# Rotary embedding on one core: the queue on which two small tables are loaded, and their place among the large loads

## Chip, cores, metric

One core of one Trainium2 chip. The metric is the device time of one execution in microseconds (us), median of the runs. All runs quoted are in the fast state; the granted clock was 1.00 in every one of them.

DVE is the vector engine, ACT the scalar engine and SP the sync engine. SP and ACT also issue the DMAs, each on a queue of its own (the SP queue and the Activation queue): in the profile of the kernel before, one queue has 4608 packets (32 loads) and the other 5664 (32 stores and the tables); of the changed kernel, where SP issues the tables, the first has 5664 and the second 4608. Landing times are those that the profile gives. The span is the length of the one profiled execution, a little less than its device time (328.5 of 330.26 us in the kernel before).

## The reference

```python
x: (8, 2048, 16, 64) float32; cos, sin: (2048, 32) float32
x1, x2 = x[..., 0::2], x[..., 1::2]          # pairs
out1 = x1 * cos - x2 * sin
out2 = x1 * sin + x2 * cos                   # cos, sin by position, the same for batch and head
out  = interleave(out1, out2)                # same shape, float32
```

64 MB go in and 64 MB come out; the tables are 256 KB each.

## The kernel before

The work is cut into 32 tiles of 128 partitions x 4096 floats (2 MB). For each tile: a load of x on the SP queue, a cast to bf16 on ACT (`halve`), three DVE operations (`rotate`), a cast back on ACT and a store on the Activation queue (`store`). There are five buffers for x, four for the output and two for each bf16 tile between them.

```python
    cos_t = cos.rearrange("(g p k) c -> p g (k c)", p=P, k=K)   # P=128, K=4: runs of 512 B
    sin_t = sin.rearrange("(g p k) c -> p g (k c)", p=P, k=K)
    xpool = ctx.enter_context(tc.tile_pool(name="xpool", bufs=NX))      # NX = 5
    opool = ctx.enter_context(tc.tile_pool(name="opool", bufs=4))
    ...  # cut: other pools and tiles
    def load(i):
        ...
        nc.sync.dma_start(out=xt, in_=x_t[b, g])
    ...  # cut: halve, rotate
    def store(i):
        ...
        nc.scalar.copy(out=ot, in_=rotated.pop(i))
        nc.scalar.dma_start(out=out_t[b, g], in_=ot)

    with tc.manual_schedule():
        load(0)
        nc.scalar.dma_start(out=cos_sb, in_=cos_t)
        nc.scalar.dma_start(out=sin_sb, in_=sin_t)
        for i in range(1, NX):
            load(i)
        ...  # cut: three DVE operations make s_tab and c_tab from sin_sb and cos_sb
        halve(0)
        for i in range(n):                    # n = 32
            if i + 1 < n:
                halve(i + 1)
            rotate(i)
            store(i)
            if i + NX < n:
                load(i + NX)
```

The trace adds something that the source doesn't say: the sixth and the seventh load of x wait for the tables, with which they share no data. The SP queue waits 20.1 us for cos and 10.8 us for sin, and these loads are issued at 23.46 and 34.66 us, right after cos and sin land (23.43 and 34.61). Why the program waits there is not shown by the runs. The prediction calls these two the lane waits.

## Time and profile before

| | before |
|---|---|
| median time | 329.98 us (329.90 to 330.17) |
| span of the profiled run | 328.5 us |
| DVE, ACT busy | 66%, 70% |
| moved by DMA | 134.76 MB, 410 GB/s over the span |
| cos, sin: issue to landing | 22.7, 33.4 us |
| first store issued | 46.4 us |

The number to look for is DMA traffic over time; the prediction shows the slices and stretches. Here only the waits that change sides later: engine and line, what it waited for, us in total, times, longest.

```profile
ACT ot L91 <- DMA out_dram<-ot: 36.0, 18, 2.3
...
ACT xh L60 <- DMA xt<-in_x_dram: 7.1, 2, 5.6
```

ACT waits mostly for a free output buffer, that is, for a store to land, and hardly ever for x.

### The profile page before, as it was taken

Reading aid. Unit: us, or ns where it says so; the run is one execution under the profiler, and the core shown is the slowest. Engines: PE = TensorE matmul, PEld = TensorE weight load, DVE = VectorE, ACT = ScalarE, POOL = GpSimd, SP = SyncE. Lnnn points to the kernel's source line nnn. Section 1 sums busy time; section 2 is a strip of 40 time slices with the busy share of each in tenths; the row PEclk is TensorE's granted clock in tenths of the full one; section 3 lists DMA queues with packets and bytes.
Section 4 is the critical chain, followed back from the end, with each engine's and each line's share of the span. In section 5 each row is a group of like instructions: output and inputs, shape, how many; then the busy total and the mean of one; then the engine's idle time right before and its main releaser. Section 6 shows DMA issues by size and latency. Waiting matters only on the chain.

```text
span 328.5 us, 334 instructions
## 1 busy us (share of the span) xinstructions
DVE 218.3 (66%) x99; ACT 230.8 (70%) x65; POOL 0.2 (0%) x4
## 2 busy tenths in 40 slices
DVE  0000798899999999866668866667876666876910
ACT  1710079999999999676786676687677678669740
POOL 0000000000000000000000000000000000000000
DMA  7999739999999999999999999999999999999997
GB/s 295 427 423 425 268 140 353 405 427 435 427 435 429 437 425 437 424 435 427 436 427 435 427 435 429 433 429 433 429 433 429 433 429 433 429 435 427 435 427 315
DMA packets 10275, 134.76 MB, mean 410 GB/s; under 512 B 1057, under 2 KB 2081, under 8 KB 2081
## 3 DMA queue, kind: packets, MB, share of 16 engines
q1 hardware_dynamic: 4608, 67.11, 48.7%
q10 hardware_dynamic: 5664, 67.64, 48.4%
q14 instruction: 3, 0.02, 0.0%
HBM read 67.63 MB, written 67.11 MB: 410 GB/s over the span
## 4 chain that ended last, share of the span: by engine, by line
DMA 62%; ACT 24%; issue 5%; DVE 4%; ACTq 1%
DMA out_dram<-ot 52%; ACT ot L91 18%; DMA sin_sb<-in_sin_dram 10%; ACT xh L60 6%; DVE pt L85 1%; DVE qt L79 1%; DVE pt L80 1%; ACTq L92 1%; ACTq L96 0%; DVE s_tab L102 0%; DVE s_tab L103 0%; ACTq L91 0%; DVE c_tab L104 0%
## 5 line engine op out<-in xcount | busy, mean ns | idle before, releaser
L91 ACT CAST ot<-pt 128x4096 f32<-128x4096 bf16 x32 | 115.3, 3604 | 64.7 <-DMA out_dram<-ot 36.0
L60 ACT CAST xh<-xt 128x4096 bf16<-128x4096 f32 x32 | 115.4, 3605 | 19.5 <-ACT ot L91 12.4
L79 DVE TENSOR_TENSOR qt<-xh,s_tab 128x4096 bf16<-128x4096 bf16 x32 | 73.3, 2291 | 59.2 <-ACT xh L60 59.2
L85 DVE TENSOR_TENSOR pt<-pt,qt 128x4096 bf16<-128x4096 bf16 x32 | 73.3, 2292 | 1.1
L80 DVE TENSOR_TENSOR pt<-xh,c_tab 128x4096 bf16<-128x4096 bf16 x32 | 73.1, 2284 | 0.0
L102 DVE CAST s_tab<-sin_sb 128x512 bf16<-128x512 f32 x1 | 0.5, 454 | 34.6 <-DMA sin_sb<-in_sin_dram 34.6
L60 ACT ACT_TABLE_LOAD x1 | 1.3, 1283 | 1.8 <-issue 1.8
L104 DVE CAST c_tab<-cos_sb 128x1024 bf16<-128x1024 f32 x1 | 0.7, 684 | 0.0
L103 DVE TENSOR_SCALAR s_tab<-sin_sb 128x512 bf16<-128x512 f32 x1 | 0.4, 442 | 0.0
L130 POOL MEMSET const-bfloat16-1.0<- 128x1 bf16 x1 | 0.1, 102 | 0.0
L130 POOL MEMSET const-uint8-127<- 128x1 uint8 x1 | 0.1, 102 | 0.0
L130 POOL MEMSET const-float32-0.0<- 128x1 f32 x1 | 0.1, 99 | 0.2 <-issue 0.2
L130 POOL MEMSET const-float32-1.0<- 128x1 f32 x1 | 0.1, 99 | 0.0
## 6 DMA issues: line engine op xcount, KB each, us to landing
xt<-in_x_dram SPq DMA_DIRECT2D x32, 2048.0 KB, 31.0
out_dram<-ot ACTq DMA_DIRECT2D x32, 2048.0 KB, 32.0
cos_sb<-in_cos_dram ACTq DMA_DIRECT2D x1, 256.0 KB, 22.7
sin_sb<-in_sin_dram ACTq DMA_DIRECT2D x1, 256.0 KB, 33.4
```

The lines of the kernel that those rows point to most:

```text
L60: nc.scalar.copy(out=xh, in_=loaded.pop(i))
L79: nc.vector.tensor_tensor(out=rows(qt), in0=rows(xh), in1=tab(s_tab), op=mult)
L80: nc.vector.tensor_tensor(out=rows(pt), in0=rows(xh), in1=tab(c_tab), op=mult)
L85: nc.vector.tensor_tensor(out=pt3, in0=pt3, in1=q_swap, op=add)
L91: nc.scalar.copy(out=ot, in_=rotated.pop(i))
L92: nc.scalar.dma_start(out=out_t[b, g], in_=ot)
L102: nc.vector.tensor_copy(out=s2[:, :, 0], in_=sin_flat)
L103: nc.vector.tensor_scalar_mul(s2[:, :, 1], sin_flat, -1.0)
L104: nc.vector.tensor_copy(out=c_tab.rearrange("p g k (i j) -> p (g k i) j", j=2), in_=cos_sb.rearrange("p g c -> p (g c)").to_broadcast([P, ...
L130: nc = _bacc.Bacc("TRN2", target_bir_lowering=False, num_devices=1)
```

## The change

The intent is to get the tables in sooner: on the SP queue they stand behind the first load of x and ahead of the second, so the first rotation need not wait until 36 us.

```diff
         load(0)
-        nc.scalar.dma_start(out=cos_sb, in_=cos_t)
-        nc.scalar.dma_start(out=sin_sb, in_=sin_t)
+        nc.sync.dma_start(out=cos_sb, in_=cos_t)
+        nc.sync.dma_start(out=sin_sb, in_=sin_t)
         for i in range(1, NX):
             load(i)
```

## The prediction

> **What bounds the kernel now.** I read the page first: busy shares, the slices, the chain.
>
> ```profile
> DVE 218.3 (66%) x99; ACT 230.8 (70%) x65; POOL 0.2 (0%) x4
> ...
> DMA  7999739999999999999999999999999999999997
> GB/s 295 427 423 425 268 140 353 405 427 435 427 435 429 437 425 437 424 435 427 436 427 435 427 435 429 433 429 433 429 433 429 433 429 433 429 435 427 435 427 315
> ...
> DMA 62%; ACT 24%; issue 5%; DVE 4%; ACTq 1%
> ```
>
> No compute engine is above 70%, while the DMA engines stand at 9 in nearly every slice: the kernel is bound by its 134.76 MB of traffic. The one hole is in slices 5 and 6 (33 to 49 us). So only microseconds without DMA traffic can be won. Next, the table of stretches (start:end, length, busy time and count of three engines, clock, DMA share, GB/s):
>
> ```profile
> 0.00:8.00 8.00, 0.00 (x0) 1.28 (x1) 0.20 (x4) 1.00 0.78 293
> 8.00:32.00 24.00, 0.00 (x0) 7.21 (x2) 0.00 (x0) 1.00 1.01 423
> 32.00:48.00 16.00, 13.30 (x9) 4.81 (x2) 0.00 (x0) 1.00 0.53 202
> 48.00:60.00 12.00, 10.25 (x5) 11.56 (x4) 0.00 (x0) 1.00 0.97 354
> 60.00:120.00 60.00, 54.10 (x25) 56.72 (x17) 0.00 (x0) 1.00 1.01 432
> 120.00:320.00 200.00, 140.63 (x63) 149.25 (x42) 0.00 (x0) 1.00 1.01 431
> 320.00:328.50 8.50, 0.00 (x0) 0.00 (x0) 0.00 (x0) 1.00 0.73 314
> ```
>
> Full rate is 431 GB/s. I count each stretch's shortfall as length x (1 - rate/431): start 2.6, then 0.5, hole 8.5, ramp 2.1, none from 60 to 320, end 2.3. Together 16.0 us; with 134.76 MB / 431 = 312.7 us that is 328.7, the span (328.5) within rounding.
>
> Why the hole? The timeline of the start and the waits of the SP queue up to 47 us:
>
> ```profile
> 34.63 0.45 DVE L102 CAST s_tab<-sin_sb 128x512 bf16<-128x512 f32 x1 [34.63 <-DMA sin_sb<-in_sin_dram]
> ...
> 35.91 2.28 DVE L79 TENSOR_TENSOR qt<-xh,s_tab 128x4096 bf16<-128x4096 bf16 x1
> ...
> 46.39 0.37 ACTq L92 DMA_DIRECT2D out_dram<-ot  x1
> ```
> ```profile
> SPq L55 <- DMA cos_sb<-in_cos_dram: 20.1, 1, 20.1
> SPq L55 <- DMA sin_sb<-in_sin_dram: 10.8, 1, 10.8
> ```
>
> The 256 KB sin table lands only at 34.6 us, so the first rotation starts at 35.9 and the first store at 46.4. There is also a less visible wait: the sixth and seventh loads of x sat in the SP queue until cos and sin had landed. [...]They issued at 23.46 and 34.66; the eighth load needs a buffer that only the third halving frees, at 50.4. Hence a dip at 33 to 37, and nothing at all from 42 to 46.
>
> [...]4608 packets for 32 loads is 144 each, 9 per engine[...]. cos is 512 runs of 512 B, 32 packets per engine. Turn about, cos ends after 32 x packets, that is four loads; with cos itself 8.65 MB. The windows show about 8.9 MB moved by the landing of cos at 23.4 us. A table packet pays for 16 KB of x each time. [...]Here, by the reading above, the issuer sets the order in which the bytes come. [...]In the window up to 46 us the ACT queue's 1056 packets took 3.9% of 16 engines, 1.8 us per engine for 66 packets, 27 ns each; at 431 GB/s their bytes would take 1.2 us.
>
> **The change, part by part.**
>
> *Removed.* Two issues (0.47 and 0.53 us) from the ACT queue. ACT then waits for x anyway: nothing. The turn-taking goes: with one queue in use, the tables' packets stand behind the first load and ahead of the second.
>
> *Added.* Two issues on SP, about 1 us; the first load's 4.9 us of transfer covers them. The second load has to wait for the tables' 64 packets per engine, 64 x 27 ns = 1.7 us, bytes that had to be moved in any case.
>
> *Moved: the start.* The first load landed at 8.4; without small packets between (8 x 27 ns) 8.2. sin lands at about 8.2 + 1.7 + 0.1 = 10.0. The DVE tables took 1.28 us from 34.63 to 35.91, so they are ready at 11.3, while the first halving runs 8.4 to 12.0 (3.6 us). First rotation 12.05 (was 35.91), three DVE operations at 2.3 to 18.9, the second halving (x lands at about 14.8) to 18.6, first output cast 19.0 to 22.6, first store issued at about 22.7 (was 46.4). The pipeline starts 23.7 us earlier.
>
> [...]the sixth load [...]issues at about 12; the seventh [...]issues after the second halving, at about 18.7. Loads queue until the first stores join: the hole closes.
>
> *What it is worth.* Not 23.7 us, for DMA is busy during most of that time. The hole of 8.5 us goes entirely. The ramp of 2.1 us (48 to 60) is a stretch in which store and load each have about one transfer under way; in the changed kernel loads are several deep by then, so I take 1.6 of it. Back come two costs. First, the tables in one lump, with no 16 KB packets to overlap with: I choose 0.5 us.
>
> Second, the end. Today seven loads are done before the first store[...]; at the end about seven stores remain, enough to cover the last tile's compute. In the changed kernel stores begin at 23.4, when x landed at 8.2, 14.8, 19.7 and would at 24.6: a lead of only 3.7. After the last load lands (time 0): halve to 3.6, rotate to 10.5, cast to 14.1, issue and first data 15.2 (0.7 us from issue to data at the first store of the trace). At time 0 some 1.7 stores are in the queue, 8.4 us at 4.87 each (2.097 MB / 431); the next-to-last store, issued at 7.6, follows to 13.3. So the DMA engines stand still from 13.3 to 15.2: 1.9 us, which I count as new.
>
> Sum for the span: 328.5 - 8.5 - 1.6 + 0.5 + 1.9 = 320.8. The median time exceeds the span by 330.0 - 328.5 = 1.5, so 322.3 us by this sum. I shade it to 321.8, since the lead grows whenever the store queue runs dry for a moment, and then the gap at the end shrinks. That is 2.5% less.
>
> With the smaller lead the steady wait should change sides too: with a lead under about six, ACT waits for xt before a halving and no longer for an output buffer. DMA stays full either way.
>
> **The rivals.**
>
> *A: the whole earlier start counts* (23.7 us, about 306). For it: the chain of waits gives sin's load 10% of the span. Against: 312.7 us of pure traffic[...]. I rule it out.
>
> *B: the gain is given back at the end, or the ramp stays.* If the ramp's loss stays whole and the end costs 4 us instead of 1.9, the time is 322.3 + 1.6 + 2.1 = 326, within 2%. For it: the lead of 3.7 is just short of what the last tile needs. Against: a store queue that runs dry hands its turns to the loads, which widens the lead again, so the gap should not grow much beyond half a transfer.
>
> *C: the tables are slow by themselves*, because 1024 small packets in a row are limited by making or fetching them, not by sharing. If cos really needs its 22.7 us, the second load stands behind both and the time goes to about 345. Against: 27 ns per packet, and the count of 8.65 MB that turn-taking predicts. If a packet alone took 80 ns, the tables would take 5.1 us, 3.4 more: 325.
>
> *D: nothing moves*, because the loads filled the start anyway. Against: the hole is idle time on the bounding resource, and only late tables and the two lane waits cause it.
>
> **Range and chances.** The line of 2% is at 323.4. The hole alone gives 321.5 when nothing is paid back; hole and ramp give 319.4; a full end gap and a slow lump give 325. Range 319.3 to 325.2. Faster by over 2%: 0.72. Within 2%: 0.27. Slower: 0.01, for C.
>
> **What would show it right or wrong.** Right: sin lands at 9 to 12 us; first store issued at 22 to 24; sixth load issued near 12; every slice from the second to the last but one at 9; waits of SP for cos and sin gone; first 60 us at over 400 GB/s; waits of ACT for xt where those for output buffers were; a gap of 1 to 3 us just before the last store's transfer. Wrong: a slow stretch after 8 us (C), a new hole between 12 and 40 us, a rate below 431 in the middle (each 1% is 3 us), or an end gap beyond 4 us (B).

Where the prediction speaks of turns, these figures of the trace of the kernel before stand behind it. By the counts of its profile a load or store of 2 MB is 144 packets, 128 of 16 KB and 16 of under 512 B; the two tables are 1024 packets of 512 B and 32 of under 512 B. From 4 to 22 us, with loads on one queue and tables on the other, the SP queue moved 499 packets (7.39 MB) and the Activation queue 497 (0.25 MB). With nothing on the other queue, loads moved at 426 GB/s (38 to 40 us) and stores at 426 (320 to 322 us). The 80 ns under rival C is an assumption.

## The result, and the profile after

319.88 us (319.76 to 319.95, 4 runs) against 330.0 for the kernel before in the same rounds: ratio 0.9692, 95% interval 0.9676 to 0.9709, 3.1% less. (A ratio is the mean time of one kernel's fast runs over that of the other's of the same rounds, so not quite the ratio of the medians quoted.)

The page of the changed kernel: the slices of DMA and the chain that ended last.

```profile
DMA  7999999999999999999999999999999999999997
GB/s 272 418 429 431 431 429 431 435 433 435 435 431 429 429 431 429 428 431 429 428 433 439 433 431 435 431 429 429 431 429 429 431 429 429 439 431 437 429 435 307
...
DMA 78%; ACT 13%; DVE 4%; issue 2%; ACTq 1%; SPq 0%
```

The hole in slices 5 and 6 is gone: every slice but the first and the last stands at 9. The table of stretches, columns as in the prediction:

```profile
0.00:8.00 8.00, 0.00 (x0) 1.28 (x1) 0.20 (x4) 1.00 0.75 273
8.00:32.00 24.00, 20.05 (x12) 19.28 (x6) 0.00 (x0) 1.00 1.03 427
32.00:48.00 16.00, 14.53 (x7) 15.18 (x5) 0.00 (x0) 1.00 1.01 433
48.00:60.00 12.00, 10.56 (x6) 11.59 (x4) 0.00 (x0) 1.00 1.01 431
60.00:309.50 249.50, 173.28 (x77) 180.84 (x52) 0.00 (x0) 1.00 1.01 431
309.50:317.80 8.30, 0.00 (x0) 0.89 (x1) 0.00 (x0) 1.00 0.76 322
```

Shortfall against 431 GB/s, as length x (1 - rate/431):

| | before | after |
|---|---|---|
| 0 to 8 | 2.6 | 2.9 |
| 8 to 32 | 0.4 | 0.2 |
| 32 to 48 | 8.5 | 0 |
| 48 to 60 | 2.1 | 0 |
| 60 to the end | 2.3 | 2.1 |
| sum | 16.0 | 5.2 |

(The sums are of unrounded terms.) The difference, 10.8 us, is the difference of the spans (328.5 - 317.8 = 10.7) within rounding. The timeline of the start:

```profile
10.30 0.46 DVE L102 CAST s_tab<-sin_sb 128x512 bf16<-128x512 f32 x1 [10.30 <-DMA sin_sb<-in_sin_dram]
...
12.22 2.29 DVE L79 TENSOR_TENSOR qt<-xh,s_tab 128x4096 bf16<-128x4096 bf16 x1 [0.55 <-ACT xh L60]
...
22.71 0.37 ACTq L92 DMA_DIRECT2D out_dram<-ot  x1
```

sin lands at 10.3 instead of 34.6, and the first store is issued 23.7 us earlier (22.71 against 46.39). Less than half of that appears in the time. And the waits of ACT have changed sides:

```profile
ACT xh L60 <- DMA xt<-in_x_dram: 75.3, 28, 6.6
```

### The profile page after: what moved, and what is told of

It is laid out like the page before. It is cut to its first block, busy times and chain, and to the rows that moved or that the text cites. A ratio compares the mean times of both kernels' runs of the same rounds, so it can differ in the third digit from the quotient of the medians.

```text
span 317.8 us, 335 instructions
## 1 busy us (share of the span) xinstructions
DVE 218.4 (69%) x99; ACT 229.1 (72%) x65; POOL 0.2 (0%) x4
## 4 chain that ended last, share of the span: by engine, by line
DMA 78%; ACT 13%; DVE 4%; issue 2%; ACTq 1%; SPq 0%
DMA xt<-in_x_dram 78%; ACT ot L91 7%; ACT xh L60 7%; DVE pt L85 1%; DVE qt L79 1%; DVE pt L80 1%; ACTq L92 1%; SPq L55 0%
## 5 line engine op out<-in xcount | busy, mean ns | idle before, releaser
L60 ACT CAST xh<-xt 128x4096 bf16<-128x4096 f32 x32 | 115.4, 3605 | 76.9 <-DMA xt<-in_x_dram 75.3
L102 DVE CAST s_tab<-sin_sb 128x512 bf16<-128x512 f32 x1 | 0.5, 461 | 10.3 <-DMA sin_sb<-in_sin_dram 10.3
```

The lines of the kernel that those rows point to most:

```text
L60: nc.scalar.copy(out=xh, in_=loaded.pop(i))
L102: nc.vector.tensor_copy(out=s2[:, :, 0], in_=sin_flat)
```

## The experiments

Three questions: is it the queue, or what competes with the tables? Does the earlier start count, or only traffic that would have been missing? What happens at the end? Twelve kernels ran, each correct and each in 3 rounds against the kernel before (330.1 to 330.2 in all of them).

### Where the tables stand on the SP queue: pos0, pos3, pos5

```diff
-        load(0); cos; sin; load(1) .. load(4)      # the changed kernel
+        cos; sin; load(0) .. load(4)               # pos0
+        load(0) .. load(2); cos; sin; load(3), load(4)   # pos3
+        load(0) .. load(4); cos; sin               # pos5
```

> Theory (only the moments without DMA traffic count; the tables must be there before the first seven loads of x run out at about 38.5 us): the tables land first, x0 lands about 1.8 us later than in the changed kernel (about 10.2 instead of 8.4), the first store is issued at about 24.4 instead of 22.7, and the time does not change: 319.9, within 0.5. Rival (the start of the pipeline is itself on the path): 1.7 us slower, 321.6.

> Tables on the SP queue behind the third load of x. By bytes ahead of them (6.82 MB at 427 GB/s after a start loss of 2.9 us, and 0.7 to landing) sin lands at about 19.6, the first store is issued at about 31.4, still before the seven loads run out at 38.5. Theory: no hole, 319.9 within 0.5, although the pipeline starts 9 us later. Rival (every microsecond of a later start counts): about 329.

> Tables on the SP queue behind the fifth load. sin lands at about 29.4 and the first store is issued at about 41.2, its data from 41.9; the seven loads run out at 38.5. Theory: a hole of about 3.4 us and up to 2 us of slow ramp, 323.3 to 325.3. Rival 1 (the SP queue itself is what helps): 319.9. Rival 2 (every microsecond of a later start counts): about 338.

| | sin landed | first store issued | time | ratio to before |
|---|---|---|---|---|
| pos0 | 4.5 | 26.1 | 322.00 | 0.9753 |
| changed kernel | 10.3 | 22.7 | 319.88 | 0.9692 |
| pos3 | 20.0 | 31.8 | 319.93 | 0.9689 |
| pos5 | 30.1 | 41.8 | 325.52 | 0.9858 |

pos3 starts its stores 9 us later than the changed kernel and takes the same time: the earlier start as such is worth nothing. pos5 has the tables on the "good" queue, but too late. Two stretches of pos5 show the hole and the ramp again:

```profile
32.00:48.00 16.00, 14.94 (x7) 9.36 (x3) 0.00 (x0) 1.00 0.79 323
48.00:60.00 12.00, 11.23 (x6) 11.18 (x4) 0.00 (x0) 1.00 0.96 366
```

16 x (1 - 323/431) + 12 x (1 - 366/431) = 5.8 us; the time is 5.6 us over that of the changed kernel. That is 0.2 us above the range I gave it.

pos0 missed: I expected no change, it is 2.1 us slower, and the rival's number (321.6) was the closer one. Its reason doesn't hold, though, since pos3 starts later still. The stretches of pos0 show where the time went:

```profile
0.00:8.00 8.00, 1.36 (x3) 1.28 (x1) 0.20 (x4) 1.00 0.69 211
8.00:25.00 17.00, 9.33 (x5) 9.72 (x3) 0.00 (x0) 1.00 1.01 429
25.00:32.00 7.00, 5.97 (x3) 6.55 (x3) 0.00 (x0) 1.00 1.01 393
```

By 8 us it has moved 211 x 8 = 1.69 MB and the changed kernel 273 x 8 = 2.18 MB; that is 1.2 us at full rate. Another 0.6 us is missing between 25 and 32, and 0.4 us more than in the changed kernel at the end (10.4 us at 329 GB/s). These are about the 2.1 us, so it is missing traffic again, over half of it at the start. The first halving starts at 12.0, not 10.2 as I expected. The trace shows two parts of that: with loads of x queued since 1.77, DMA moved only 150, 311 and 246 GB/s in the three microseconds from 4 to 7; and by 12.0 it had moved 3.34 MB, 0.7 MB more than the tables and the first load hold, so part of the second load was moved before the first had landed. Why either happens is left open.

### The queue or the competition: act_alone and sp_shared

```diff
 # act_alone: kernel before (tables on Activation); sp_shared: changed kernel (tables on SP); in both:
         for i in range(1, NX):
-            load(i)                    # on SP
+            load(i, nc.scalar)         # on Activation
```

> Tables on the Activation queue as in the kernel before, but loads two to five of x are issued on the same queue behind them; only the first load is on SP. Theory (order of bytes, not the queue's name): the tables take turns with the first load only, sin lands at 9 to 11 us, no hole, 319.9 within 0.7. Rival (the Activation queue is slow for such tables): sin lands after 20 us and the time is above 325.

> Tables on the SP queue between the first load and the sixth, but loads two to five of x on the Activation queue, beside them. Theory: turn-taking comes back. All 40 x packets per engine of the first five loads go out beside or ahead of the tables; once those have run out the rest of the tables goes through alone: sin lands at about 28 to 29 us, first store at about 40, a hole of 2 to 3 us and some ramp: 322.5 to 325. Rival (SP as the issuer is what helps): sin at about 10, 319.9.

The DMA issues of the tables, first in act_alone, then in sp_shared (queue, count, size, us from issue to landing):

```profile
cos_sb<-in_cos_dram ACTq DMA_DIRECT2D x1, 256.0 KB, 8.5
sin_sb<-in_sin_dram ACTq DMA_DIRECT2D x1, 256.0 KB, 8.8
```
```profile
cos_sb<-in_cos_dram SPq DMA_DIRECT2D x1, 256.0 KB, 27.9
sin_sb<-in_sin_dram SPq DMA_DIRECT2D x1, 256.0 KB, 28.2
```

act_alone: tables on the Activation queue, yet sin landed at 10.1 and the time is 319.95 (ratio 0.9689). sp_shared: tables on SP, yet sin landed at 29.8, the first store was issued at 41.6 and the time is 325.1 (0.9846), 0.1 above its range. So the name of the queue made no difference here; what mattered is whether large loads stood on the *other* queue while the tables were under way: sin landed at 10.1 and 10.3 us (act_alone, changed kernel) where only the first load of x went before or beside the tables, and at 29.8 and 34.6 (sp_shared, kernel before) where further loads went beside them.

### Are turns taken per packet? runs2k_act and runs2k_sp

```diff
-    cos_t = cos.rearrange("(g p k) c -> p g (k c)", p=P, k=K)     # 4 runs of 512 B in each partition
+    cos_t = cos.rearrange("(p g k) c -> p (g k c)", p=P, k=K)     # 1 run of 2 KB
 # sin, x and out dealt out to partitions in the same way; runs2k_act: tables on Activation as in the kernel before
```

> Kernel before (tables on the Activation queue, competing with all loads), but the rows are dealt out so that each partition's share of a table is one run of 2 KB: 8 packets per engine and table instead of 32. Theory (turns are taken per packet): cos lands after one load of x, at 8 to 9 us, sin after two, at 13 to 15, first store at about 26, no hole, 320 within 1 unless the new row spacing of x changes the full rate. Rival (turns by bytes, or the Activation queue is slow as such): sin lands at 30 us or later and the time stays at 328 or more.

> The same row order, tables on SP as in the changed kernel. Theory: within 0.5 us of the run with the tables on the Activation queue and this row order, about 319.5 (0.4 us less packet cost of the tables) unless the row spacing of x changes the full rate of 431 GB/s. Rival (the queue matters): at least 3 us between the two.

The DMA issues of runs2k_act (queue, count, size, us from issue to landing):

```profile
cos_sb<-in_cos_dram ACTq DMA_DIRECT2D x1, 256.0 KB, 8.1
sin_sb<-in_sin_dram ACTq DMA_DIRECT2D x1, 256.0 KB, 13.2
```

Same bytes, same queue, same competitors as in the kernel before, only a quarter of the packets (256 of 2 KB for the two tables instead of 1024 of 512 B): 8.1 and 13.2 us from issue to landing instead of 22.7 and 33.4, one load of x for each table, as counted in advance. The time is 319.63 (0.968) on the Activation queue and 319.78 (0.9687) on SP. The edit also deals out the rows of x and out anew; that by itself changes nothing, for runs2k_sp takes the time of the changed kernel (319.78 against 319.88). So a second cure for the same illness cost nothing here: longer runs.

### The two waits for the tables: lanes, lanes_free

```diff
 # lanes (kernel before, and):
         nc.scalar.dma_start(out=cos_sb, in_=cos_t)
+        nc.scalar.dma_start(out=spare0, in_=x_t[0, 0][0:16, 0:128])
         nc.scalar.dma_start(out=sin_sb, in_=sin_t)
+        nc.scalar.dma_start(out=spare1, in_=x_t[0, 0][0:16, 0:128])
 # lanes_free (kernel before, and):
             store(i)
+            if i == 0:
+                nc.scalar.dma_start(out=spare, in_=x_t[0, 0][0:16, 0:128])
```

> The kernel before, but [...]the sixth and seventh loads of x no longer wait for cos and sin. Theory: these loads issue at about 12.2 and 18.8 and go on taking turns with sin, so sin lands LATER, at about 38.5 (all seven loads out), the first store goes out at about 50.3, and DMA stands still in one piece of about 12 us instead of pieces of 8.5 in sum: about 333.5, 332 to 335. Rival (the two waits[...] made part of the hole, so taking them away helps): below 329.

> Second try at the kernel before without the two waits[...] (in the first try the extra loads stood behind cos in the Activation queue, landed with it, and the two loads of x waited for them instead, until 24.2 and 34.9). Now one extra small load on the Activation queue directly behind the first store[...]. Theory: loads six and seven issue at about 12.3 and 17.5, sin lands LATER than before, at 38 to 39 instead of 34.6, the first store goes out at about 50.4, DMA stands still for some 12 us in one piece instead of 8.5 in sum: 333 to 335. Rival (the two waits made part of the hole): below 329. Second rival (sin lands at 34.6 as before): 330.

lanes told nothing about its question: 330.32 (1.0003) where I expected 332 to 335, since the extra loads stood behind cos on the same queue and the two loads of x now waited for them (25.6 us together, until 24.22 and 34.85). lanes_free did remove the waits: the sixth and seventh loads were issued at 12.06 and 17.21 instead of 23.46 and 34.66. It got *slower*: 335.17 (1.0155), 0.2 above the range I gave it. Its timeline and its stretches:

```profile
39.49 0.45 DVE L104 CAST s_tab<-sin_sb 128x512 bf16<-128x512 f32 x1 [39.49 <-DMA sin_sb<-in_sin_dram]
...
51.25 0.36 ACTq L94 DMA_DIRECT2D out_dram<-ot  x1
```
```profile
32.00:48.00 16.00, 8.48 (x7) 0.39 (x1) 0.00 (x0) 1.00 0.41 170
48.00:60.00 12.00, 10.50 (x5) 10.64 (x4) 0.00 (x0) 1.00 0.68 263
```

The two loads now went beside sin, which landed 4.9 us later (39.5 against 34.6), and so the first store was 4.9 us later. The shortfall of these stretches is 9.7 + 4.7 = 14.4 us against 10.6 before, 3.8 of the 4.5 us between the spans (333.0 and 328.5). (The small extra load is part of the edit; its issue on ACT takes 0.44 us, and I didn't measure its cost apart.) The accidental waits had done the kernel a service. A wait that stands out in the profile of a queue need not be the one that costs; here what those loads would have displaced was on the path.

### The end: end_after, end_before, end_pos3

```diff
         nc.vector.tensor_tensor(out=rows(qt), in0=rows(xh), in1=tab(s_tab), op=mult)
+        if i == n - 1:
+            for _ in range(2):          # superfluous, same result
+                nc.vector.tensor_tensor(out=rows(qt), in0=rows(xh), in1=tab(s_tab), op=mult)
```

> Changed kernel with two superfluous DVE multiplies (2.29 us each, same result) in the last tile only. Reading of the profile: the last store is issued at 310.42, its data could begin at about 311.1, and the one before it ends at about 311.2 (316.1 less one transfer of 4.87), so the slack at the end is near 0.1 us. Theory: nearly all of 4.6 us appears, 324.2 to 324.6. Rival (the end is covered by a queue of stores with room to spare): 319.9.

> Kernel before with the same two multiplies in the last tile. There the last store is issued at 316.86, data from 317.6, and the store before it ends at about 321.3: slack about 3.7 us. Theory: only about 0.9 of 4.6 us appears, 330.4 to 331.2. Rival (the last tile is on the path in both kernels): 334.6.

> Tables behind the third load, plus the two superfluous multiplies (4.6 us) in the last tile. Without them this version takes 319.9, as the changed kernel does, but its stores start 9 us later, so more stores are left at the end: its last store is issued at 306.1, data from about 306.8, and the one before it ends at about 310.9: slack about 4.1. Theory: 0 to 0.8 of 4.6 us appears, 319.9 to 320.7. Rival (the end is on the path in every version with a full DMA): 323.7, as in the changed kernel with the same multiplies.

Of 4.6 us added to the last tile, 3.8 appeared in the changed kernel (323.67 against 319.88), 0.3 in the kernel before (330.42 against 330.16) and none in pos3 (319.86 against 319.93). For end_after I had expected 4.3 to 4.7. Microsecond by microsecond, the end of end_after:

```profile
310.00:311.00 1.00, 0.73 (x1) 0.23 (x1) 0.00 (x0) 1.00 0.73 311
311.00:312.00 1.00, 0.00 (x0) 1.00 (x1) 0.00 (x0) 1.00 0.04 16
312.00:313.00 1.00, 0.00 (x0) 1.00 (x1) 0.00 (x0) 1.00 0.00 0
313.00:314.00 1.00, 0.00 (x0) 1.00 (x1) 0.00 (x0) 1.00 0.00 0
314.00:315.00 1.00, 0.00 (x0) 0.37 (x1) 0.00 (x0) 1.00 0.00 0
315.00:316.00 1.00, 0.00 (x0) 0.00 (x0) 0.00 (x0) 1.00 1.19 508
```

All other stores are out at about 311 and DMA waits for the last tile. So the mechanism of the end, as the prediction had it, exists: an early first store leaves fewer stores to cover the last tile. In the other two kernels the slack is 4 us or more. In the changed kernel the 0.8 us that didn't appear (4.6 - 3.8) is not all slack, as its last halving and last store show beside those of end_after:

```profile
296.30 3.60 ACT L60 CAST xh<-xt 128x4096 bf16<-128x4096 f32 x1 [2.61 <-DMA xt<-in_x_dram]
...
310.42 0.34 ACTq L92 DMA_DIRECT2D out_dram<-ot  x1
```
```profile
295.62 3.60 ACT L60 CAST xh<-xt 128x4096 bf16<-128x4096 f32 x1 [2.62 <-DMA xt<-in_x_dram]
...
314.40 0.34 ACTq L95 DMA_DIRECT2D out_dram<-ot  x1
```

From the last halving to the last store it is 18.8 us against 14.1, so all of the added work is in; but in the one profile of each the last load landed 0.7 us earlier in end_after, for a reason that the runs don't show, and the store was issued only 4.0 us later. The slack itself is thus some 0.2 us (4.0 - 3.8), near the 0.1 that I had read off. For the changed kernel this is the edge: I estimate that further work in the last tile would be paid nearly in full.

## Why the prediction was right, and where a size was off

The measured 319.88 lies in the range (319.3 to 325.2), in its lower part; 321.8 was 1.9 too high, and the gain was 10.1 where I had said 8.2.

- **DMA traffic is the bound, only its absence costs.** Right. The shortfalls account for both spans, and pos3, with a 9 us later start and the same time, shows it. Rival A (306) fell. That there was no rate to gain above 431 GB/s was my assumption and is not shown; the ten versions whose stretches I asked for moved 430 to 432 GB/s in every stretch of 60 us or more after the first 60.
- **The tables are late because they share turns packet by packet.** Right for this kernel: 499 packets of the one queue went with 497 of the other (4 to 22 us, kernel before). act_alone and sp_shared separate competition from the queue (sin at 10.1 and 29.8 us), and runs2k_act (sin at 14.4) changes the packets and, by the control runs2k_sp, nothing else that counts.
- **The dates of the start.** Right: sin 10.3 (said 10.0), first rotation 12.22 (12.05), first store 22.71 (22.7), sixth and seventh loads 12.21 and 18.82 (12 and 18.7). One reading was 0.2 off: the first load landed at 8.6 in the kernel before (7.9 after its issue), not at 8.4. Between 8.5 and 9.0 us, with the first load out and the second not begun, the tables alone moved at 345 GB/s (346 packets, none of 2 KB or more), against 426 for a load in runs of 16 KB alone (38 to 40 us, kernel before), so rival C (tables slow by themselves) fell.
- **The hole, -8.5.** Right: it went entirely. What I said of the two lane waits in this connection was half wrong. I listed them (rival D) among the causes of the hole; lanes_free shows that without them it is larger (9.7 us of shortfall from 32 to 48 us instead of 8.5).
- **The ramp, -1.6.** It went entirely, -2.1.
- **The lump of the tables, +0.5.** The first 32 us show 3.1 us of shortfall against 3.0, so +0.1.
- **The gap at the end, +1.9.** This is the step that failed in size: the end fell short by 2.1 us, before by 2.3, so nothing new, and the gap of 1 to 3 us that I had named as a sign of being right is not there (from 310 to 312 us DMA fell 0.2 us short). After the last load of x had landed (296.3), DMA ran at 423 GB/s for 19.9 us more, which is 8.42 MB or 4.0 stores, where I had a lead of 3.7. I had counted loads by their landing; by bytes, 372 GB/s x 23.4 us less the tables is 8.18 MB, 3.9 loads. The rest was 0.4 us in the last store's issue, 14.1 us after that landing instead of 14.5. A third of a store is 1.5 us, so the gap closed. That end_after pays 3.8 of 4.6 us shows how near it was. The shading by 0.5 us had named this effect, a lead that grows, but at a quarter of its size. Rival B (326) fell on the same point.
- **The shift of the waits.** Right for the changed kernel: ACT waits 75.3 us for x and none for output buffers. But it costs nothing: pos3 waits 39.3 us for output buffers, as the kernel before does, and takes the same time. My threshold for it (a lead under about six) was too coarse: pos3 had 297 x 8 + 24 x 418 GB/s by 32 us, less the tables, 5.7 loads, and still waits for buffers. And the lead is not all that decides: act_alone issues its first store at 22.6 with the changed kernel's lead (277 x 8 + 426 x 15.3 GB/s less the tables, 3.9 loads), yet its ACT waits 47.5 us for output buffers and 10.5 for x, and it takes the same time (319.95). In it stores and four of the first loads share a queue.

Of the 1.9 us between 321.8 and the result, the end gap is by far the largest term. In the other direction, execution by execution the time exceeds the span by 2.0 us here (319.76 and 317.8) and by 1.8 before (330.26 and 328.5). My 1.5 set a median against the span of a single execution, and I had taken it as constant.

No version beat the changed kernel clearly. runs2k_act has the lowest median, 319.63, 0.25 below; they did not run in the same rounds, and their ratios to the kernel before (0.968 and 0.9692) have overlapping intervals. The 5.2 us that remain are the start and the end.

## What to carry to other kernels

A small table that everything waits for should not be loaded on one queue while large loads run on the other, if the trace shows what it showed here: packet for packet (499 and 497), so that 256 KB in runs of 512 B took 22.7 us beside runs of 16 KB and 8.1 us in runs of 2 KB. Put it on the queue of the large loads, ahead of all that the first tile doesn't need but behind that tile's own load (in front of it cost 2.1 us here), or lay it out in longer runs. In a kernel bound by traffic, add up the microseconds without traffic before and after; a start that is earlier by 24 us was worth 10, and a visible wait was worth less than nothing.
